# A hybrid RWKV-7 and attention block on one core: the sums of squares of the down projections move to the place where these are projected, and the recurrence's output is split into a dead half of the hidden state during attention

## The chip, the core and the metric

The kernel runs on one core of a Trainium2 chip. The metric is device time in microseconds (us) from start to end of one execution. TensorE is called PE here, its weight loads PEld, VectorE DVE, ScalarE ACT, GpSimd POOL; SP is the engine that issues nearly all DMAs, and each engine works through its instructions in the order in which they stand in its own queue.

## What is computed

One layer on 256 latent tokens (`x`) and 256 context tokens (`ctx`), width 2048, everything in fp32. The lines of the reference that matter:

```python
hm = rmsnorm(h, norm_w) * (1 + scale) + shift          # per stream
rkv, z_r, wd, ad, q_dn, kv_dn, k_rope, z_m, gates = split_in(hm @ w_in)

# branch 1: RWKV-7 recurrence over the tokens, both directions, 16 heads -> o_rw (1024 wide)
# branch 2: multi-head latent attention, 8 heads
q  = (rmsnorm(q_dn, q_norm_w) @ w_uq)                  # q_dn is 512 wide
kv = (rmsnorm(kv_dn, kv_norm_w) @ w_ukv)               # kv_dn is 256 wide
k  = concat(k_nope, broadcast(k_rope))                 # k_rope is 64 wide
q, k = rmsnorm(q, q_gain), rmsnorm(k, k_gain)          # then rotary, softmax, o_ml = att * silu(z_m)

x_new = x + g * (sigmoid(g_r) * (o_rw @ w_br_r) + sigmoid(g_m) * (o_ml @ w_br_m)) @ w_out
```

Three row norms need sums of squares over rows of a down projection: of `q_dn`, of `kv_dn`, and of `k_rope` (as a part of the norm of `k`). These sums are what the first half of the change moves.

## The kernel before

**Tiles and number format.** The hidden state `hm` lies transposed in SBUF, as 16 tiles of 128 features by 512 tokens (256 latent tokens in columns 0 to 255, 256 context tokens in columns 256 to 511). It is kept as a pair of fp32r tensors, a rounded high part `hmh` and the remainder `hml`. Every weight block is loaded (`w`, 128x1024, three buffers), and each half of it split in the same way by ACT (`wh`, a cast) and DVE (`wl`, a subtraction), three buffers each. A product is then three matmuls (`mm3`, line 221): high by high, high by low, low by high. `acc<-hmh,wh` and its two sisters in the profile are such matmuls of the input projection; below they are called projection matmuls. All recorded work runs through two helper classes, so nearly every instruction has the line L103 (matmul), L107 (transpose) or L122 (elementwise).

**Stages.** (1) Modulation, norm and the first six projection tiles. (2) The recurrence of branch 1: two chains of small steps (`front_chain` and `back_chain`) with finishing steps and a block inversion as further queues. `drive` (line 505) writes them in the order in which a small clock model expects their operands, and whenever no chain is ready it advances a generator `bg` (line 1032), the background, by one step. The background holds the rest of the input projection: the tiles that the recurrence needs next, and then the list `extra`: 24 tiles of merge gates, two tiles of `kv_dn` (`kv_g`, line 470), `k_rope` (`kr_g`, line 479), four tiles of `q_dn` (`q_g`, line 475), eight of `z_m` (`zm_g`) and the last eight merge gates. A background step is two to six projection matmuls. (3) Attention, lines 1077 to 1336, in six stages. Stage 0 runs `down()` (line 1135), stages 1 to 4 `up(hp)` for a pair of heads (queries, keys and values), stages 2 to 5 `attend(hp)` for the pair that `up` finished one stage earlier. In each round every generator of the stage takes a step, and then the background takes on average `BGM = 1.3` steps (`BG0 = 8` in stage 0). So projection matmuls fill PE's waits in all stages until they run out. (4) The merge: o_rw and o_ml by `w_br`, tile by tile, gated and summed. (5) The product with `w_out` and the residual.

**What `down()` does.** While it projects, the kernel writes the down projections to DRAM: `spill` (line 464) copies 256 columns from PSUM with ACT into a tile `th` (tag `th`, two buffers, shared with all the other generators) and lets SP store it to `kvd`, `krd` or `qdd`. `krd` has 128 rows, since `kr_g` leaves two partial sums in the upper and lower 64 partitions. After the recurrence, `down()` loads `kvr`, both halves of `krd` and `qdr`, adds the halves on DVE, squares everything on ACT into a double-buffered tile `sq`, and sums over the features with 20 small matmuls into one PSUM tile `pss` (each takes 128 columns of `sq` as its weights and two columns of ones as its data). From `pss` come the row norms: an inverse square root by integer tricks and three Newton steps on DVE (`rsqrt`, 11 small instructions), then `spread`, which multiplies a diagonal matrix `dg` by ones to bring the norms onto all partitions. With them `kvr` is scaled and split into `kvh`, `kvl`; `qdr` is scaled by its gain and split into `qnh`, `qnl`; and `krw` is transposed, rotated and doubled to `krS`.

**The end of the recurrence, and the merge.** The recurrence writes its output `y` per pair of heads to DRAM (`orwd`, 128x8x256). After attention the merge loads all of it (`orw`, two DMAs of 512 KB) and splits it into `ob0h`, `ob0l`, and `omla`, the attention's output, into `ob1h`, `ob1l`. Both are needed by the first merge tiles.

**What lies in the dead half.** After the last projection that reads context tokens, columns 256 to 511 of `hmh` and `hml` are not read as hidden state any more. `attend` keeps the transposed softmax weights `PT` there: head `hh` uses four of the 16 feature tiles, at `4 * (hh % 4)`.

Of the kernel before, what the change touches and what calls it, by code (L numbers as in the profile page):

```python
# [16 lines left out]
P = 128  # L17
# [109 lines left out]
def hybrid_block(  # L127
# [74 lines left out]
    def halfs(pool, shape, name, bufs=2):  # L202
        return [pool.tile(shape, F32R, name=name + c, tag=name + c, bufs=bufs) for c in "hl"]
# [247 lines left out]
    krd = dr1.tile([P, TT], F32, name="krd")  # L451
# [12 lines left out]
    def spill(dst, ps):  # L464
        th = wp.tile([P, T], F32, name="th", tag="th", bufs=2)
        t = th[0:dst.shape[0]]
        S.copy(t, ps)
        nc.sync.dma_start(dst, t)

    def kv_g(i):  # L470
        ps = yield from proj_g(76 + i, TT)
        for j in range(2):
            spill(kvd[:, i, T * j:T * j + T], ps[:, T * j:T * j + T])

    def q_g(i):
        spill(qdd[:, i], (yield from proj_g(72 + i, T)))
        done.add(("q", i))

    def kr_g():
# [16 lines left out]
        for j in range(2):  # L496
            spill(krd[:, T * j:T * j + T], ps[:, T * j:T * j + T])
# [52 lines left out]
    with tc.tile_pool(name="rw", bufs=1) as rw:  # L550
# [29 lines left out]
        def wk():  # L580
            return pp.tile([P, 512], F32, name="wk", tag="wk", bufs=2)
# [489 lines left out]
    omla = late.tile([P, 8, T], F32, name="omla")  # L1071


    with tc.tile_pool(name="ml", bufs=2) as ml:
# [60 lines left out]
        def down():  # L1135
# [3 lines left out]
            nc.sync.dma_start(krw, krd[0:64])  # L1139
            krw2 = ml.tile([64, TT], F32, name="krw", tag="Pm")  # L1140
            nc.sync.dma_start(krw2, krd[64:128])
            qdr = ml.tile([P, 4, T], F32, name="qdr", tag="vfl")
            nc.sync.dma_start(qdr, qdd)
            pss = wk()
            for k in range(2):
                sq = ml.tile([P, TT], F32, name="sq", tag="Pm")
                S.activation(sq, kvr[:, k], AF.Square)
                for i in range(4):
                    E.matmul(pss[:, 8 * k + 2 * i:8 * k + 2 * i + 2], lhsT=sq[:, 128 * i:128 * i + 128], rhs=ones[:, 0:2],
                             start=True, stop=True)  # L1150
            sq = ml.tile([P, TT], F32, name="sq", tag="Pm")
            V.tensor_tensor(krw, krw, krw2, ALU.add)
            S.activation(sq[0:64], krw, AF.Square)
            for i in range(4):
                E.matmul(pss[:, 16 + 2 * i:18 + 2 * i], lhsT=sq[0:64, 128 * i:128 * i + 128], rhs=ones[0:64, 0:2],
                         start=True, stop=True)
            for j in range(2):
                sq = ml.tile([P, 2, T], F32, name="sq", tag="Pm")
                S.activation(sq, qdr[:, 2 * j:2 * j + 2], AF.Square)
                for k in range(2):  # L1160
                    for i in range(2):
                        o = 24 + 4 * (2 * j + k) + 2 * i
                        E.matmul(pss[:, o:o + 2], lhsT=sq[:, k, 128 * i:128 * i + 128], rhs=ones[:, 0:2], start=True, stop=True)
            yield

            st = ml.tile([P, 40], F32, name="st", bufs=1)
            V.tensor_copy(st, pss[:, 0:40])
            s2 = st.rearrange("p (n two) -> p n two", two=2)[:, :, 0]
# [116 lines left out]
        def attend(hp):  # L1285
            qT, qrT, kT, vf, rq, rkb = ups.pop(hp)
            for h in range(2):
# [6 lines left out]
                b = 4 * (hh % 4)  # L1294
# [30 lines left out]

        due = 0.0
        for stage in range(6):
            us = [down()] if stage == 0 else [up(stage - 1)] if stage < 5 else []
            at = [attend(stage - 2)] if stage > 1 else []
            gs = us + at  # L1330
# [184 lines left out]
```

## Time and profile before

| | |
|---|---|
| median of three runs | 1336.67 us (1335.77 to 1337.12) |
| the profiled execution's own time | 1337.52 us |
| its span in the trace | 1335.6 us |
| its mean granted PE clock | 0.981 |
| recurrence | to about 969 us of the span |
| `down()` and attention | about 970 to 1143 us |
| merge | about 1144 to 1244 us |
| last product | to the end |

How to read it: the span runs from the first to the last recorded instruction; the 1.9 us between it and the execution's own time lie around it and are not in any row. "PEclk" and the clock in the rows by stretch are the share of full speed that was granted to PE. A row of the timeline gives the start, the time, the engine, the tiles and, in brackets, how long the engine was idle before it and what ended that. Matmul rows overlap, since they are pipelined: what one costs is the distance from one start to the next.

### The profile page before, as it was taken

Reading aid. Unit: us, or ns where it says so; the run is one execution under the profiler, and the core shown is the slowest. Engines: PE = TensorE matmul, PEld = TensorE weight load, DVE = VectorE, ACT = ScalarE, POOL = GpSimd, SP = SyncE. Lnnn points to the kernel's source line nnn. Section 1 sums busy time; section 2 is a strip of 40 time slices with the busy share of each in tenths; the row PEclk is TensorE's granted clock in tenths of the full one; section 3 lists DMA queues with packets and bytes.
Section 4 is the critical chain, followed back from the end, with each engine's and each line's share of the span. In section 5 each row is a group of like instructions: output and inputs, shape, how many; then the busy total and the mean of one; then the engine's idle time right before and its main releaser. Section 6 shows DMA issues by size and latency. Waiting matters only on the chain.

```text
span 1335.6 us, 29638 instructions
## 1 busy us (share of the span) xinstructions
PE 1273.5 (95%) x11484; PEld 1057.0 (79%) x11484; DVE 958.0 (72%) x2704; ACT 618.8 (46%) x1370; POOL 3.3 (0%) x9
## 2 busy tenths in 40 slices
PE   5999989999999998999999999999989999799998
PEld 2667877788787787788787777788878888799887
DVE  4445878878777868677876887776548877677655
ACT  3445544444443544344444444544436665444443
POOL 0000000000000000000000000000000000000000
PEclk9999999999999999999999999999979999899999
DMA  9995554354352454254254232353344332577685
GB/s 380 417 418 206 181 164 130 89 171 142 78 173 64 123 163 127 56 166 132 57 110 125 72 99 80 93 151 100 107 150 123 103 103 95 189 227 234 188 270 174
DMA packets 127740, 208.12 MB, mean 156 GB/s; under 512 B 63600, under 2 KB 80752, under 8 KB 127088
## 3 DMA queue, kind: packets, MB, share of 16 engines
q1 hardware_dynamic: 127600, 206.23, 49.0%
q8 instruction: 90, 1.47, 0.5%
q14 instruction: 50, 0.41, 0.1%
HBM read 193.33 MB, written 12.85 MB: 154 GB/s over the span
## 4 chain that ended last, share of the span: by engine, by line
PE 79%; DVE 11%; DMA 6%; issue 2%; ACT 2%; SPq 0%; DVEq 0%; ACTq 0%
PE acc L103 33%; PE chp L103 17%; PE lv L103 10%; PE wk L103 6%; PE a L103 5%; PE ch L103 3%; DMA w<-in_w_proj 3%; DVE wl L122 3%; PE wk L107 2%; PE pm L103 2%; DMA wm<-in_w_mod_ss 2%; DVE BK L122 1%; ACT wh L122 1%; DVE wt L122 1%; DMA xT<-in_xcT 1%
## 5 line engine op out<-in xcount | busy, mean ns | idle before, releaser
L122 ACT CAST wh<-w 128x512 fp32r<-128x512 f32 (+1 forms) x484 | 289.1, 607 | 336.3 <-PE acc L103 182.5
L122 DVE TENSOR_TENSOR wl<-w,wh 128x512 fp32r<-128x512 f32 (+1 forms) x480 | 319.7, 674 | 134.1 <-ACT wh L122 123.8
L103 PE MATMUL acc<-hmh,wh 128*128 128x256 f32 (+1 forms) x1200 | 390.6, 325 | 0.0
L103 PE MATMUL acc<-hml,wh 128*128 128x256 f32 (+2 forms) x1200 | 370.3, 309 | 0.8 <-issue 0.8
L103 PE MATMUL acc<-hmh,wl 128*128 128x256 f32 (+1 forms) x1184 | 364.6, 308 | 0.6 <-DVE wl L122 0.5
L103 PEld LDWEIGHTS acc<-hmh,wh 128*128 128x128 f32 x1200 | 228.0, 190 | 28.7 <-issue 6.8
L103 PEld LDWEIGHTS acc<-hmh,wl 128*128 128x128 f32 x1184 | 225.3, 190 | 14.9 <-DVE wl L122 1.1
L103 PEld LDWEIGHTS acc<-hml,wh 128*128 128x128 f32 (+1 forms) x1200 | 228.0, 190 | 11.0 <-issue 0.8
L122 DVE TENSOR_TENSOR pr<-wt 64x14 f32<-64x14 f32 (+6 forms) x224 | 42.5, 190 | 4.7
L122 DVE TENSOR_TENSOR wt<-wt,pr 64x14 f32<-64x14 f32 (+6 forms) x224 | 42.3, 189 | 4.3
L122 ACT COPY UV<-Mn 64x128 f32<-64x128 f32 x112 | 33.1, 295 | 22.1 <-DVE Mn L122 18.4
L103 PE MATMUL chp<-ob0h,wh 128*128 128x256 f32 x128 | 37.4, 293 | 5.7 <-ACT ob0h L122 5.7
L103 PEld LDWEIGHTS chp<-UV,AQ 128*64 128x64 f32 (+1 forms) x512 | 24.5, 138 | 21.3 <-ACT UV L122 10.9
L103 PE MATMUL a<-hmh,wh 128*128 128x512 f32 x96 | 40.7, 424 | 0.0
L122 ACT COPY UV<-chp 64x128 f32<-64x128 f32 x64 | 16.5, 257 | 50.8 <-PE chp L103 50.6
L103 PE MATMUL chp<-UV,AQ 128*64 128x64 f32 (+1 forms) x512 | 35.9, 238 | 4.2 <-ACT UV L122 4.1
L103 PE MATMUL a<-hmh,wl 128*128 128x512 f32 x96 | 38.1, 397 | 0.4 <-DVE wl L122 0.4
L103 PE MATMUL a<-hml,wh 128*128 128x512 f32 x96 | 37.9, 395 | 0.0
L103 PE MATMUL chp<-ob0l,wh 128*128 128x256 f32 x128 | 37.4, 292 | 0.0
L122 DVE SCALAR_TENSOR_TENSOR Mn<-chp,rho,Mr 128x64 f32<-128x64 f32 x96 | 24.1, 278 | 18.2 <-PE chp L103 17.7
L103 PE MATMUL chp<-ob0h,wl 128*128 128x256 f32 x128 | 37.1, 290 | 0.0
L103 PE MATMUL chp<-ob1h,wh 128*128 128x256 f32 x128 | 36.5, 285 | 0.0
(324 smaller groups left out, 2388.1 us busy)
## 6 DMA issues: line engine op xcount, KB each, us to landing
w<-in_w_proj SPq DMA_DIRECT2D x148, 512.0 KB, 3.8
wm<-in_w_mod_ss SPq DMA_DIRECT2D x64, 512.0 KB, 9.4
w<-in_w_mod_g SPq DMA_DIRECT2D x32, 512.0 KB, 3.6
w<-in_w_br SPq DMA_DIRECT2D x32, 512.0 KB, 3.6
w<-in_w_out SPq DMA_DIRECT2D x32, 512.0 KB, 3.7
w<-in_w_first SPq DMA_DIRECT2D x16, 384.0 KB, 8.5
xT<-in_xcT SPq DMA_DIRECT2D x4, 1024.0 KB, 8.6
thd<-th SPq DMA_DIRECT2D x32, 128.0 KB, 1.8
```

What stands on the lines that cost most here:

```text
L103: return self.engine.matmul(out, lhsT=lhsT, rhs=rhs, **kw)
L107: return self.engine.transpose(*a)
L122: return fn(out, *a, **kw)
```

## The change

The sums of squares are taken at the place where the tiles are projected. `spill` becomes a generator: after the copy and its store it squares the same PSUM columns with ACT into a second `th` tile, yields, sums with two small matmuls per 256 columns into a PSUM tile `wk`, and copies four columns into a tile `sqd` that stays in SBUF. `kr_g` first adds its two partial sums (a copy of the upper 64 partitions into a `th` tile, an addition in PSUM on DVE), so that `krd` has 64 rows and one load. `down()` then only loads, and starts with the norms from `sqd`.

The split of the recurrence's output moves from the merge into attention. A new generator `bring()` runs beside `up(2)` and `attend(1)` in stage 3: eight times it loads 128x256 of `orwd` into a `th` tile and splits it into feature tiles 8 to 15 of the dead half. To make room, `attend` uses `4 * (hh % 2)`. The merge reads branch 1 from there (in the profile these merge matmuls are then `chp<-hmh,wh`) and keeps only the split of `omla`.

```diff
-    krd = dr1.tile([P, TT], F32, name="krd")
+    krd = dr1.tile([64, TT], F32, name="krd")
+
+    sqd = cst.tile([P, 40], F32, name="sqd")
...
-    def spill(dst, ps):
+    def spill(dst, ps, col):
+
         th = wp.tile([P, T], F32, name="th", tag="th", bufs=2)
-        t = th[0:dst.shape[0]]
-        S.copy(t, ps)
-        nc.sync.dma_start(dst, t)
+        n = dst.shape[0]
+        S.copy(th[0:n], ps)
+        nc.sync.dma_start(dst, th[0:n])
+        sq = wp.tile([P, T], F32, name="th", tag="th", bufs=2)
+        S.activation(sq[0:n], ps, AF.Square)
+        yield
+        pss = pp.tile([P, 512], F32, name="wk", tag="wk", bufs=2)
+        for i in range(2):
+            E.matmul(pss[:, 2 * i:2 * i + 2], lhsT=sq[0:n, 128 * i:128 * i + 128], rhs=con("ones")[0:n, 0:2], start=True, stop=True)
+        V.tensor_copy(sqd[:, col:col + 4], pss[:, 0:4])
...
         for j in range(2):
-            spill(krd[:, T * j:T * j + T], ps[:, T * j:T * j + T])
+            ts = slice(T * j, T * j + T)
+            low = wp.tile([P, T], F32, name="th", tag="th", bufs=2)
+            S.copy(low[0:64], ps[64:P, ts])
+            V.tensor_tensor(ps[0:64, ts], ps[0:64, ts], low[0:64], ALU.add)
+            yield from spill(krd[:, ts], ps[0:64, ts], 16 + 4 * j)
...
+    ob = [[t[:, 8:16, T:TT] for t in (hmh, hml)]]
...
-            nc.sync.dma_start(krw, krd[0:64])
-            krw2 = ml.tile([64, TT], F32, name="krw", tag="Pm")
-            nc.sync.dma_start(krw2, krd[64:128])
+            nc.sync.dma_start(krw, krd)
...
-            pss = wk()
-            for k in range(2):
-                sq = ml.tile([P, TT], F32, name="sq", tag="Pm")
-                S.activation(sq, kvr[:, k], AF.Square)
...
-            V.tensor_copy(st, pss[:, 0:40])
-            s2 = st.rearrange("p (n two) -> p n two", two=2)[:, :, 0]
+            s2 = sqd.rearrange("p (n two) -> p n two", two=2)[:, :, 0]
...
-                b = 4 * (hh % 4)
+                b = 4 * (hh % 2)
...
+        def bring():
+
+            for p in range(8):
+                th = wp.tile([P, T], F32, name="th", tag="th", bufs=2)
+                nc.sync.dma_start(th, orwd[:, p])
+                yield
+                split(th, *(t[:, p] for t in ob[0]))
+                yield
...
-            gs = us + at
+            gs = us + at + ([bring()] if stage == 3 else [])
...
-    ob = [halfs(mg, [P, 8, T], f"ob{b}", 1) for b in range(2)]
-    orw = mg.tile([P, 8, T], F32, name="orw", bufs=1)
-    for b in range(2):
-        for q in range(2):
-            qs = slice(4 * q, 4 * q + 4)
-            if not b:
-                nc.sync.dma_start(orw[:, qs], orwd[:, qs])
-            split((omla if b else orw)[:, qs], ob[b][0][:, qs], ob[b][1][:, qs])
+    ob.append(halfs(mg, [P, 8, T], "ob", 1))
+    for q in range(2):
+        qs = slice(4 * q, 4 * q + 4)
+        split(omla[:, qs], *(t[:, qs] for t in ob[1]))
```

**How the instructions stand now.** Three places carry the prediction.

ACT's queue in the recurrence, where the first `kv_dn` tile is spilled (`th` is the spill's tile, `acc` its PSUM source, `UV`, `Y`, `wt` belong to the recurrence's chains), before:

```order
L122 CAST wh<-w 128x512
L122 COPY th<-acc 128x256 x2
L122 COPY UV<-chp 64x128
L122 CAST wh<-w 128x512
L122 COPY wt<-wt 64x256
```

Both copies stand in a row here, one in each of the two `th` buffers. The same place of ACT's queue in the changed kernel, where `ACTIVATE th<-acc` is the new square:

```order
L122 CAST wh<-w 128x512
L122 COPY th<-acc 128x256
L122 ACTIVATE th<-acc 128x256
L122 COPY UV<-chp 64x128
L122 COPY th<-acc 128x256
L122 COPY Y<-chp 128x128
L122 ACTIVATE th<-acc 128x256
L122 COPY wt<-wt 64x256
```

The second copy now needs the buffer whose store to DRAM began only two instructions earlier, and `Y` and `wt` of the recurrence stand behind it.

DVE's queue at the end of the recurrence and in `down()`, before (`krw` is the addition of the two halves, `st` the copy of the sums, `ss` the start of the norms):

```order
L122 TENSOR_TENSOR wl<-w,wh 128x512
L122 SCALAR_TENSOR_TENSOR th<-th,acc 128x256
L122 TENSOR_TENSOR krw<-krw 64x512
L122 TENSOR_SCALAR qdr<-qdr,vv 128x256 x3
L122 COPY st<-wk 128x40
L122 TENSOR_SCALAR qdr<-qdr,vv 128x256
L122 TENSOR_TENSOR wl<-w,wh 128x512 x2
L122 TENSOR_TENSOR ss<-st 128x4
```

The norms begin after all the loads and sums. DVE's queue at the same place in the changed kernel, where the norms (`rs`) are nearly done:

```order
L122 TENSOR_TENSOR wl<-w,wh 128x384
L122 SCALAR_TENSOR_TENSOR rs_y<-rs_z,rs_y 128x6
L122 SCALAR_TENSOR_TENSOR th<-th,acc 128x256
L122 TENSOR_TENSOR wl<-w,wh 128x512
L122 SCALAR_TENSOR_TENSOR rs_z<-rs_y 128x6
L122 TENSOR_TENSOR rs_z<-rs_z,ss 128x6
L122 SCALAR_TENSOR_TENSOR rs<-rs_z,rs_y 128x6
L122 TENSOR_TENSOR rs_12592<-rs 128x2
L122 TENSOR_TENSOR dg<-cc,rs 128x512
L122 TENSOR_SCALAR qdr<-qdr,vv 128x256 x4
L122 SCALAR_TENSOR_TENSOR kvr<-kvr,vv,wk 128x512 x2
L122 TENSOR_TENSOR qnl<-qdr,qnh 128x1024
```

The norms moved ahead of everything that waits for a load; PE's `spread` of `dg` now follows 92 projection matmuls after the last transposes of the recurrence (`chp<-cc,rvb`), where 102 stood there ahead of the first sums before.

ACT's queue for the last pair of heads, before (`Pm` is the exponential, `hmh` the copy of transposed weights into the dead half, `wh` the split of a weight block for projection or merge matmuls):

```order
L122 CAST wh<-w 128x512
L122 ACTIVATE Pm,sm<-Pm,sm 128x512
L122 CAST wh<-w 128x512
L122 ACTIVATE Pm,sm<-Pm,sm 128x512
L122 CAST hmh<-wk 128x4x128
L122 CAST wh<-w 128x512
L122 ACTIVATE th<-acc 128x256
L122 CAST hmh<-wk 128x4x128
```

Weight splits stand between the softmax steps, so PE has projection matmuls to do. ACT's queue at the same place in the changed kernel:

```order
L122 CAST qrTh<-wk 128x512
L122 ACTIVATE Pm,sm<-Pm,sm 128x512 x2
L122 CAST hmh<-wk 128x4x128 x2
L122 ACTIVATE Pm,sm<-Pm,sm 128x512 x2
L122 CAST hmh<-wk 128x4x128 x2
L122 CAST obh<-omla 128x1024
L122 CAST wh<-w 128x512
```

No weight split is left between them: stage 3 has more rounds than before, since `bring()` takes 16 steps, each round takes background steps, and the background is used up when the last pair of heads begins. Before, 64 projection matmuls stood in PE's queue from the last `dg` to the end of attention; now none does there, but 24 merge matmuls of branch 1 follow the last pair.

More of the change, by code (lines that the diff above doesn't have):

```diff
@@ L472, in kv_g @@
         for j in range(2):
-            spill(kvd[:, i, T * j:T * j + T], ps[:, T * j:T * j + T])
+            yield from spill(kvd[:, i, T * j:T * j + T], ps[:, T * j:T * j + T], 8 * i + 4 * j)
     def q_g(i):
-        spill(qdd[:, i], (yield from proj_g(72 + i, T)))
+        yield from spill(qdd[:, i], (yield from proj_g(72 + i, T)), 24 + 4 * i)
         done.add(("q", i))
@@ L1138, in down @@
             krw = ml.tile([64, TT], F32, name="krw", tag="Pm")
-            nc.sync.dma_start(krw, krd[0:64])
-            krw2 = ml.tile([64, TT], F32, name="krw", tag="Pm")
-            nc.sync.dma_start(krw2, krd[64:128])
+            nc.sync.dma_start(krw, krd)
             qdr = ml.tile([P, 4, T], F32, name="qdr", tag="vfl")
             nc.sync.dma_start(qdr, qdd)
-            pss = wk()
-            for k in range(2):
-                sq = ml.tile([P, TT], F32, name="sq", tag="Pm")
-                S.activation(sq, kvr[:, k], AF.Square)
[L1148 to L1163, printed above, removed]
             yield
-            st = ml.tile([P, 40], F32, name="st", bufs=1)
-            V.tensor_copy(st, pss[:, 0:40])
-            s2 = st.rearrange("p (n two) -> p n two", two=2)[:, :, 0]
+            s2 = sqd.rearrange("p (n two) -> p n two", two=2)[:, :, 0]
             V.tensor_tensor(ss[:, 0:4], s2[:, 0:4], s2[:, 4:8], ALU.add)
```

## Prediction

> **What bounds the kernel now.** I read the page's busy times first, then what PE waited for, then the two places where its clock falls.
>
> ```profile
> PE 1273.5 (95%) x11484; PEld 1057.0 (79%) x11484; DVE 958.0 (72%) x2704; ACT 618.8 (46%) x1370; POOL 3.3 (0%) x9
> PEclk9999999999999999999999999999979999899999
> ```
>
> PE is busy for 95% of the span, so PE's work and what stops or slows PE set the time. PE's clock falls in two of the 40 slices: at `down()` and where the merge begins. Both are what the change touches. PE's longest wait in each place (total, times, longest):
>
> ```profile
> PE wk L103 <- issue: 2.7, 1, 2.7
> PE chp L103 <- ACT ob0h L122: 5.7, 1, 5.7
> ```
>
> The clock costs more than the waits. PE alone, by stretch: length, busy time and records, granted clock, DMA.
>
> ```profile
> 977.35:980.76 3.41, 0.71 (x7) 1.00 1.00 332
> 980.76:984.17 3.41, 3.40 (x16) 0.50 0.92 347
> 991.00:994.41 3.41, 2.50 (x10) 0.50 0.00 0
> 994.41:997.83 3.42, 3.37 (x14) 0.50 0.50 141
> 997.83:1001.24 3.41, 3.41 (x20) 1.00 0.03 12
> 670.15:673.56 3.41, 1.91 (x17) 1.00 0.45 97
> 1141.19:1144.60 3.41, 1.64 (x12) 1.00 0.21 79
> 1144.60:1148.01 3.41, 0.00 (x0) 0.50 0.91 292
> 1151.43:1154.84 3.41, 3.41 (x18) 0.50 0.35 129
> ```
>
> The clock changes on a grid of 3.41 us. Stretches busy for 21% and 48% are followed by half clock, one busy for 56% is not; 73% busy at half clock does not bring it back, a full stretch does. The Trainium skill (TensorE: Matmul & The Clock Gate, Part 1, "What's actually happening") says half rate comes after an idle window of about 3.4 us and full rate after a busy one. The grid agrees; that a window has to be idle does not, since 48% busy lost the clock.
>
> **`down()` loses its sums.** The first three rows are PE's records in 978.06 to 998.20 on projection tiles, on `sq` and on `lv`; the last gives the price of a projection matmul.
>
> ```profile
> 978.06:998.20 20.14, 4.85 (x19) 0.58 0.39 135
> 978.06:998.20 20.14, 9.14 (x40) 0.58 0.39 135
> 978.06:998.20 20.14, 1.49 (x5) 0.58 0.39 135
> 966.44:978.06 11.62, 11.62 (x102) 1.00 0.78 230
> ```
>
> Of these 20.14 us the changed kernel still has to do 19 projection matmuls at 11.62 / 102 = 0.114 and four `lv` matmuls (the fifth only begins at the edge), of 384 columns instead of 256 and so at about 0.18: 2.9 us. What goes is 17.2 us: idle PE, 20 sums at half clock, and the rest at half clock. **-17.2.**
>
> **The sums come back in the recurrence.** The nearest row is a sum of the same form, `ysq`, between two projection matmuls.
>
> ```profile
> 960.96 0.28 PE L103 MATMUL acc<-hmh,wl 128*128 128x256 f32 x1
> 961.15 0.61 PE L103 MATMUL chp<-cc,ysq 128*128 128x2 f32 x4
> 961.62 0.36 PE L103 MATMUL acc<-hmh,wh 128*128 128x256 f32 x1
> 800.00:890.00 90.00, 88.29 (x938) 72.82 (x934) 68.19 (x204) 42.79 (x106) 0.00 (x0) 0.98 0.36 104
> kvd<-th SPq DMA_DIRECT2D x4, 128.0 KB, 1.8
> ```
>
> Two sums put 0.66 us between two projection matmuls that stand 0.11 apart otherwise: 0.55. Ten spills make 5.5 us. The recurrence's stretch that holds them (800 to 890, PE's busy time is the second number) has 1.7 us of idle PE, so between 3.8 and 5.5 is paid; I take 5.5, since the chains, and not the sums, choose when PE is idle. Then there are new waits: `kv_g` and `kr_g` each spill twice in quick succession, and the second copy on ACT waits until the store from its `th` buffer has landed, 1.8 us after its issue; `Y` and `wt` of the recurrence, and the next weight split, stand behind it. Two or three split weight halves of 12 or 24 projection matmuls cover some 2 us for PE. Without that cover it is four waits of about 1 us: 0 to 4, I take 1, near the covered end, because ACT is busy for 42.79 of the 90 us only. `sqd`'s copies (four columns) and the squares hide beside PE, since both engines have room in that row. **+6.5, from 3.8 to 9.5.**
>
> **What is late next in `down()`.** Nothing there waits for a sum any more; it waits for loads and for DVE.
>
> ```profile
> 973.93 0.58 SPq L1143 DMA_DIRECT2D qdr<-qdd  x1
> DMA to landing us min/median/max: 6.3/6.3/6.3
> 974.58 2.29 DVE L122 TENSOR_TENSOR wl<-w,wh 128x384 fp32r<-128x384 f32 x4 [1.52 <-ACT wh L122]
> 979.33 0.68 DVE L122 TENSOR_TENSOR krw<-krw 64x512 f32<-64x512 f32 x1 [2.13 <-DMA krw<-krd]
> 988.77 0.62 DVE L122 TENSOR_SCALAR qdr<-qdr,vv 128x256 f32<-128x256 f32 x2 [8.76 <-ACT sq L122]
> 993.84 1.04 ACT L122 CAST qnh<-qdr 128x1024 fp32r<-128x1024 f32 x1 [1.43 <-DVE qdr L122]
> 1003.67 0.15 DVE L122 TENSOR_TENSOR rs<-rs 128x2 f32<-128x2 f32 x1
> 1003.75 0.69 DVE L122 TENSOR_TENSOR dg<-cc,rs 128x512 f32<-128x512 f32 x1
> ```
>
> In before's times: 92 projection matmuls after the transposes end at 966.44 + 92 x 0.114 = 976.9. The `dg` stands behind the four weight splits, which end at 976.9 because a weight load lands at 974, and behind one `th` (0.4), some five small steps (0.15 to 0.2 each) and itself (0.7): about 979.0. `krw` lands at 979.3 at the latest, sooner now by the second `krw` load, gone from the queue. PE idles 2.1 us. Then `spread`, the transposes and 11 projection matmuls run to 981.7. `qdr` is there at 973.9 + 6.3 = 980.2; four scalings (1.2) and `qnh` (1.0) end at 982.4 if it lands then, at 982.0 with one load fewer: 0.3. `qnl` stands behind two scalings of `kvr` (0.7 each) and takes 1.2: 0.5; the next weight splits behind it: 0.5; the rotation of `krw`: 0.3. Sum 3.7 us idle, from 2 (loads sooner) to 7 (a weight load late in SP's queue behind `kvr`, `krw`, `qdr` and a store of `zmd`, which waits for DVE). The first gap loses the clock if 1.7 of its 2.1 us lie in one window: (3.41 + 2.1 - 2 x 1.7) / 3.41, 6 of 10 positions of the grid, taking the grid's place as chance; one window at half costs 1.7, two cost 3.4: 1.3 on the mean. **+5.0, from 2 to 10.**
>
> **The merge.**
>
> ```profile
> 1143.20 0.42 DVE L122 SCALAR_TENSOR_TENSOR omla<-gm,chp 128x256 f32<-128x256 f32 x1 [1.66 <-PE chp L103]
> 1143.65 4.09 DMA orw<-orwd
> 1148.86 0.58 PE L103 MATMUL chp<-ob0h,wh 128*128 128x256 f32 x1 [5.70 <-ACT ob0h L122]
> L122 ACT CAST ob1h<-omla x2: 1039/1042/1044, 1143.7 to 1144.7; 128x1024 fp32r<-128x1024 f32 x2
> L122 DVE TENSOR_TENSOR ob1l<-omla,ob1h x2: 1220/1222/1225, 1144.8 to 1145.9; 128x1024 fp32r<-128x1024 f32 x2
> ```
>
> The chain of waits runs through the load of `orw` and its split: 5.7 us of idle PE, then 6.0 us at half clock (1148.86 to the edge at 1154.84), 3.0 lost. Now 18 merge matmuls of branch 1 follow at once (18 x 0.114 = 2.1 us), while `omla` and the first half of its split take 0.4 + 1.0 + 1.2 = 2.7: 0.7 idle. Clock losses go into the last term. -8.7 + 0.7 = **-8.0.**
>
> **`bring()` in stage 3.**
>
> ```profile
> 1056.00:1089.00 33.00, 32.83 (x223) 29.42 (x223) 26.41 (x77) 20.92 (x48) 0.00 (x0) 1.00 0.33 102
> ```
>
> Eight casts on ACT and as many subtractions on DVE, each of a quarter of the columns of `ob1h`'s and at about the 0.42 of `omla`'s row: some 3.3 us on each engine, in a stage where DVE idles 6.6 us of 33 (third busy time) and ACT 12. Eight loads join SP's queue, and each waits for one of two `th` buffers with weight loads and gate loads behind it; the three weight buffers cover that. If neither cover holds it is 3.3. Nothing is removed in this stage, so nothing is gained. **+0.6, from 0 to 3.3.**
>
> **The last pair of heads has no filler.** The rows: before's stretch from the last `dg`, a score's last matmul, the first product with the values behind it.
>
> ```profile
> 1119.49:1143.17 23.68, 9.55 (x66) 1.00 0.32 103
> 1125.42 0.39 PE L103 MATMUL chp<-krS,qrTl 128*128 128x512 f32 x1
> 1136.30 0.39 PE L103 MATMUL chp<-krS,qrTl 128*128 128x512 f32 x1
> 1140.88 0.39 PE L103 MATMUL chp<-hmh,vfh 128*128 128x256 f32 x1 [0.68 <-ACT hmh L122]
> ```
>
> From the end of a head's second score (1136.69) to its first value product is 4.2 us of maximum, exponential, normalization, transposes and split on DVE and ACT; the first score lies 1.2 ahead, and DVE takes the first tile's steps between (0.2). So 5.6 us pass from first score to values, in which PE has 1.2 + 2 x 0.5 us of work now. With values, next head's score (2.5) and the second head to its end (5.6 + 2.1) that is 15.8 us, where before took 1143.17 - 1125.81 = 17.4; ahead of it stood eight more projection matmuls, 0.9, of which about 0.5 is saved. The stretch shrinks by 2.1 us, but its 64 projection matmuls (7.3 us) were done earlier: +5.2 idle, from 4 to 7. Clock: per head, 3 us idle of about 4.5; windows that begin from 0.2 before to 2.6 after the first score's end hold 1.7 us of idle PE, 8 of 10 positions, and 73% at half does not restore the clock. One loss costs 1.7 to 3.4; two, the second running into the merge: 3.5, from 1.5 to 6. **+8.7, from 5.5 to 13.**
>
> **Sum.** -17.2 + 6.5 + 5.0 - 8.0 + 0.6 + 8.7 = -4.4. The profiled execution took 1337.5, 0.9 over the median: 1333.1, or **1332.3** against the median of 1336.67.
>
> **Rivals.**
> *Slower: the `th` buffers.* All spills, the gates and `bring()` share two. If a spill held the recurrence's chain on ACT or the `wk` PSUM tiles that its front half needs, PE would wait up to 1.8 us for each of ten. 7 us decide, 0.7 a spill; at 1.1 a spill the time is 1332.3 - 1 + 11 = 1342. For it: `Y`, `wt` and weight splits stand behind the second copy. Against it: the idle 1.7 us in 90.
> *No change: half clock through the whole last pair.* PE's 9 us of work there take 18, of which the idle time hides about half, and the merge starts at half: some 5 more, 1337.3. For it: five stretches in a row at half in `down()`. Against it: the value products and scores between are a full stretch.
> *No change: the loads hold `down()` as long.* If they land 5 us later: 1337. Against it: DMA idles after 984.
> *Much faster: the clock holds.* Without both clock terms, 1.3 + 3.5 less: 1327.5. For it: the stretch at 56%, which held; the new gaps come in pieces of 0.3 to 2.1 us. Against it: the stretch at 48%, which did not. The rule of the Trainium skill's page above, taken as it stands, speaks for this rival, since no gap here is a whole idle window.
>
> **How the numbers follow.** A measurement of this kernel can tell about 0.2%, 2.7 us, from no change: faster is below 1334.0, slower above 1339.3. The forecast has 0.58 (0.50 of it faster, 0.08 same; own range 1329.5 to 1335.3), the `th` rival 0.10 (slower), half clock throughout 0.15 (0.14 same, 0.01 slower), the loads 0.03 (same), the clock that holds 0.14 (faster): 0.64, 0.25, 0.11. The range 1326.5 to 1338.5 leaves out the `th` rival and the far ends of the others.
>
> **What would show it.** Right: `sq` gone from PE's waits after the recurrence, an idle PE of about 4 us between the transposes and `krS`; ten `wk` sums in 800 to 900; no wait of 5 us ahead of the merge; new PE waits on `Pm`, `hmh` for the last two heads, with half clock there. Wrong: PE waits on `th`, `UV` or `wk` of several us in the recurrence, or full clock in the last pair.

## The result, and the profile after

The changed kernel takes 1328.7 us (median of five runs, 1327.3 to 1333.0), the kernel before beside it 1337.1 (1335.8 to 1341.8). The ratio is 0.9936, interval 0.9911 to 0.9961: 8.4 us less, with 5 to 12 in the interval. The profiled execution took 1329.92 us, its span is 1328.1. Forecast were 1332.3 us, in a range of 1326.5 to 1338.5.

The page of the changed kernel, engines and granted clock in 40 slices:

```profile
PE 1271.5 (96%) x11484; PEld 1053.2 (79%) x11484; DVE 961.1 (72%) x2720; ACT 620.2 (47%) x1383; POOL 3.3 (0%) x9
PEclk9999989999999999899999999999999999999999
```

The slice of `down()`, a 7 before, is a 9 now (90% or more), and so is the one where the merge begins, an 8 before. To see where the time went I cut both spans at the same five events: first spill, last transposes of the recurrence, first score on `krS`, last `dg`, last `omla`, end. PE alone; length, busy time and records, clock, DMA share, GB/s. Before:

```profile
799.70:966.20 166.50, 164.16 (x1839) 0.99 0.37 105
966.20:1031.10 64.90, 57.96 (x367) 0.87 0.45 141
1031.10:1118.30 87.20, 86.83 (x585) 1.00 0.32 99
1118.30:1143.20 24.90, 23.49 (x162) 1.00 0.33 101
1143.20:1335.60 192.40, 182.29 (x1152) 0.97 0.69 219
```

After:

```profile
802.10:976.70 174.60, 173.79 (x1892) 1.00 0.36 104
976.70:1023.10 46.40, 42.81 (x302) 1.00 0.58 184
1023.10:1119.60 96.50, 95.91 (x654) 1.00 0.38 115
1119.60:1144.30 24.70, 17.75 (x99) 0.93 0.10 32
1144.30:1328.10 183.80, 178.40 (x1146) 1.00 0.72 224
```

The lengths cannot be compared as they stand, since the background's projection matmuls are not in the same stretches: 667, 203, 190, 76 and none before, 697, 187, 250, 5 and none after. With 0.114 us for each of them (the prediction's price) the stretches read, at equal numbers of projection matmuls:

| stretch | length, after less before | projection matmuls | at equal projection matmuls | forecast |
|---|---|---|---|---|
| to the first spill | +2.4 | about equal | +2.4 | 0 |
| recurrence from the first spill | +8.1 | +30 | +4.7 | +6.5 |
| to the first score (`down()`) | -18.5 | -16 | -16.7 | -17.2 + 5.0 = -12.2 |
| stages to the last `omla` | +9.1 | -11 | +10.4 | +0.6 + 8.7 = +9.3 |
| merge and last product | -8.6 | 0 | -8.6 | -8.0 |

No edit touches the part ahead of the first spill, except that 14 small chain matmuls stand ahead of it and two projection matmuls behind it. In the fourteen traces of this case it ends anywhere between 792.4 and 802.1 us, at 799.6 us in another execution of the changed kernel; so I count the first row as scatter, whose cause is open. Other matmuls changed places too: seven of the first queries (`lv`, 384 columns, 0.18 us each) and two of the first scores (0.23 each), 1.7 us in all, stand ahead of the first score on `krS` before and behind it after, and eight merge matmuls (0.9 us) stand ahead of the last `omla` after. With these the third row is -15.0, the fourth +7.8 and the fifth -7.7.

What PE waited for in the two places, `down()` and then the last pair with the merge (total, times, longest):

```profile
PE wk L103 <- issue: 1.4, 1, 1.4
PE wk L107 <- DVE kr L122: 1.2, 1, 1.2
PE wk L107 <- DVE Pm L122: 4.3, 4, 1.5
PE chp L103 <- ACT hmh L122: 2.0, 3, 0.7
PE chp L103 <- DVE obl L122: 0.7, 1, 0.7
```

No wait on `sq` is left in `down()`, and the 5.7 us ahead of the merge are 0.7, on the split of `omla`. In exchange PE waits 6.3 us for the softmax of the last four tiles and its transposed weights: in 1119.60 to 1144.30 it does 99 matmuls and is idle for 6.95 us, where it did 162 and was idle for 1.41.

### The profile page after: what moved, and what is told of

It reads as the page before. It is cut to its first block, busy times and chain, and to the rows that moved or that the text cites. A ratio compares the mean times of both kernels' runs of the same rounds, so it can differ in the third digit from the quotient of the medians.

```text
span 1328.1 us, 29671 instructions
## 1 busy us (share of the span) xinstructions
PE 1271.5 (96%) x11484; PEld 1053.2 (79%) x11484; DVE 961.1 (72%) x2720; ACT 620.2 (47%) x1383; POOL 3.3 (0%) x9
## 4 chain that ended last, share of the span: by engine, by line
PE 79%; DVE 10%; DMA 6%; ACT 2%; issue 2%; SPq 1%; DVEq 0%; ACTq 0%
PE acc L103 33%; PE chp L103 17%; PE lv L103 10%; PE wk L103 6%; PE a L103 5%; PE ch L103 3%; DVE wl L122 2%; DMA w<-in_w_proj 2%; PE wk L107 2%; PE pm L103 2%; DMA wm<-in_w_mod_ss 2%; DVE BK L122 1%; ACT wh L122 1%; DMA xT<-in_xcT 1%; DVE wt L122 1%
## 5 line engine op out<-in xcount | busy, mean ns | idle before, releaser
L122 ACT ACTIVATE Mr<-Mn,rho 128x64 f32<-128x64 f32 x96 | 30.1, 342 | 15.7 <-DVE Mn L122 14.6
L103 PE MATMUL chp<-obl,wh 128*128 128x256 f32 x128 | 36.4, 284 | 0.7 <-DVE obl L122 0.7
L103 PE MATMUL chp<-hmh,wh 128*128 128x256 f32 x128 | 36.2, 283 | 0.0
L103 PE MATMUL chp<-hmh,wl 128*128 128x256 f32 x128 | 36.2, 283 | 0.0
```

Of the source, the lines that this page charges most:

```text
L103: return self.engine.matmul(out, lhsT=lhsT, rhs=rhs, **kw)
L122: return fn(out, *a, **kw)
```

## The experiments

They ran on four chips, on each of which the kernel before takes 1333.1 to 1334.7 us, not 1337; so ratios to before on the same chip are compared. The last column counts the projection matmuls that stand in PE's queue between head 7's second score and head 8's first, between head 8's two, and behind those: the filler of the last pair.

| kernel | median us | ratio to before | interval | filler at the end |
|---|---|---|---|---|
| before (its own BGM, 1.3) | 1333.1 to 1334.7 | 1 | | 25, 11, 18 |
| `r1_after`: the change again | 1326.3 | 0.9954 | 0.9937 to 0.9970 | 0, 0, 0 |
| `e1_sums`: first half alone | 1328.3 | 0.9965 | 0.9954 to 0.9975 | 24, 0, 0 |
| `e2_bring`: second half alone | 1330.8 | 0.9983 | 0.9972 to 0.9994 | 10, 0, 0 |
| `e3_nine`: `bring()` in nine steps | 1321.0 | 0.9911 | 0.9892 to 0.9931 | 24, 0, 0 |
| `e4_nosum`: the sums left out | 1326.4 | 0.9955 | 0.9940 to 0.9969 | 0, 0, 0 |
| `e7_twice`: the sums done twice | 1327.7 | 0.9958 | 0.9943 to 0.9973 | 0, 0, 0 |
| `e5_nine12`: nine steps, BGM 1.2 | 1317.2 | 0.9881 | 0.9862 to 0.9899 | 24, 6, 18 |
| `e6_bgm11`: the change, BGM 1.1 | 1316.3 | 0.9887 | 0.9868 to 0.9906 | 27, 2, 3 |
| `e8_nosum10`: no sums, BGM 1.0 | 1311.4 | 0.9830 | 0.9816 to 0.9843 | 24, 2, 10 |
| `e9_bring115`: second half, BGM 1.15 | 1323.0 | 0.9912 | 0.9898 to 0.9925 | 24, 2, 20 |
| `e10_chain12`: statistics earlier, BGM 1.2 | 1317.8 | 0.9877 | 0.9862 to 0.9892 | 24, 4, 18 |
| `e11_before115`: before, BGM 1.15 | 1326.0 | 0.9951 | 0.9932 to 0.9971 | 27, 5, 60 |

BGM is the number of background steps per round of the stages. A trace shows one execution, which can lie off its median: that of `r1_after` took 1330.3 us, of `e4_nosum` 1322.9, of `e6_bgm11` 1321.0, of `e10_chain12` 1321.2 and of `e11_before115` 1321.6. Part of this lies ahead of the first spill, so traces are compared by stretch, and gains are taken from the ratios.

### Each half alone

The first half is the changed kernel with the merge, the load of `orw` and `attend`'s four places as before; the second is the kernel before with these lines of the diff:

```diff
+    ob = [[t[:, 8:16, T:TT] for t in (hmh, hml)]]
...
-                b = 4 * (hh % 4)
+                b = 4 * (hh % 2)
...
+        def bring():
...
-            gs = us + at
+            gs = us + at + ([bring()] if stage == 3 else [])
...
+    ob.append(halfs(mg, [P, 8, T], "ob", 1))
```

Expected of the first:

> The changed kernel's first half alone: the sums of squares at the projections, while the recurrence's output is loaded and split at the merge, as before. By the prediction's own terms: -17.2 + 6.5 + 5.0 = -5.7 against before, 1331 us. By what the changed kernel's trace shows (recurrence some 5 to 7 us longer, the stretch from its end to the first score 16.7 shorter): -10 to -12, 1325 to 1327, less some 2 that the last head without filler gives back: 1327 to 1329. Rival, that the sums only moved and the merge brought the gain: 1336 to 1338.

Expected of the second:

> The second half alone: the recurrence's output joins h's dead half in stage 3, while the sums of squares are taken in the down projections' preparation, as before. By the prediction's own terms: -8.0 + 0.6 + 8.7 = +1.3, 1338 us. By the trace of the changed kernel (first score to last omla 10.5 longer, the rest 8.8 shorter): +1.7, 1338 to 1339. Rival, that the merge brought the gain: 1328 to 1330.

The first half is 4.7 us faster than before (1333.12 x 0.0035), interval 3.3 to 6.1: the prediction's terms gave 5.7, the reading of the changed kernel's trace 8 to 10, which is too much; why its rows promised more is open, since no profile of the kernel before was taken on this chip. The second half is 2.3 us faster (0.8 to 3.7), where both readings had it slower. Together they make 7.0, close to the 6.1 that the whole change is worth in `r1_after`. So the gain does not lie in the merge alone. The second half alone, last pair and then merge to the end:

```profile
1120.00:1146.30 26.30, 21.78 (x119) 0.87 0.16 51
1146.30:1329.00 182.70, 176.93 (x1146) 0.99 0.70 225
```

It still has 119 matmuls in its last pair (99 in the changed kernel) and 4.5 us of idle PE: its recurrence takes 666 projection matmuls from the background and not 697, so the background lasts a little longer. `e1_sums`, which has no `bring()`, keeps 24, 0, 0 where before keeps 25, 11, 18. So both halves use up filler, and the price of the last pair belongs to what is left in the background there, and not to `bring()` as such.

### Where the filler is left

`e3_nine` loads and splits in nine steps, so that stage 3 goes round no oftener than without `bring()`; `e6_bgm11` leaves `bring()` as it is and changes the constant; `e5_nine12` has nine steps and the constant at 1.2.

```diff
-            for p in range(8):
-                th = wp.tile([P, T], F32, name="th", tag="th", bufs=2)
-                nc.sync.dma_start(th, orwd[:, p])
-                yield
-                split(th, *(t[:, p] for t in ob[0]))
-                yield
+            last = None
+            for p in range(9):
+                th = last
+                if p < 8:
+                    last = wp.tile([P, T], F32, name="th", tag="th", bufs=2)
+                    nc.sync.dma_start(last, orwd[:, p])
+                if p:
+                    split(th, *(t[:, p - 1] for t in ob[0]))
+                yield
```

> The changed kernel with bring() in nine steps (a load and the split of the part loaded one step earlier) in place of sixteen, so that stage 3 goes round no oftener than without it and releases no extra filler: 24 projection matmuls stand again between the scores of the last pair of heads. Theory that the last pair lacks filler: its 6.6 us of idle PE fall to about 4, the half clock there may go or stay: 2.5 to 5 us faster than the changed kernel, 1324 to 1326. Rival, that filler in the last pair only delays the heads' own chain, or that bring's casts then hold the weight splits: no difference, 1328 to 1330.

> The changed kernel with BGM at 1.1 in place of 1.3 and bring() in sixteen steps as it is: 27 and 2 projection matmuls stand between the last pair's scores, 3 behind them. Theory that only the filler's place matters: 3 to 5 us faster than the changed kernel, as nine steps were, 1320 to 1322 where before takes 1333. Rival, that the sixteen steps themselves cost in stage 3 (their loads ahead of weight loads, their casts ahead of weight splits): 1323 to 1325.

> bring() in nine steps, and BGM at 1.2 in place of 1.3, so that the stages release filler more slowly: 24 and 6 projection matmuls stand between the last pair's scores and 18 behind the values, ahead of the merge. Theory that PE's idle time behind the recurrence is a matter of where filler is left: the last pair idles about 1.5 us instead of 2.9 with nine steps alone and 6.95 in the changed kernel, and the 0.7 at the merge goes: 5 to 7 us faster than the changed kernel, 1318 to 1320 where before takes 1333. Rival, that the stages then lack the filler which the last pair gets: as nine steps alone, 1321, or slower.

The changed kernel itself was run beside the last two:

> The changed kernel once more, unaltered, so that it stands beside the others on one chip. By its measured ratio of 0.9936 [0.9911, 0.9961] to before: 1324.6 us where before takes 1333.1.

The last pair's stretch, last `dg` to last `omla`, in `r1_after`, `e3_nine`, `e6_bgm11` and `e5_nine12`:

```profile
1116.60:1144.70 28.10, 21.22 (x99) 0.77 0.09 28
1110.80:1136.70 25.90, 22.99 (x139) 0.89 0.18 56
1109.80:1135.20 25.40, 22.88 (x147) 0.93 0.25 78
1106.80:1130.90 24.10, 23.01 (x158) 1.00 0.26 83
```

From row to row PE does more matmuls in less time: idle 6.9, 2.9, 2.5 and 1.1 us, clock 0.77, 0.89, 0.93, 1.00. The stages before that do not pay for it: with BGM at 1.1 PE is idle for 0.4 us from the first score to the last `dg`. Against `r1_after`, BGM at 1.1 is worth 0.0067 x 1333 = 8.9 us, nine steps with BGM at 1.2 9.7, and nine steps alone 5.7, each with some 3.4 us of uncertainty either way. All three gained more than was expected of them, `e6_bgm11` beyond the uncertainty (3 to 5 expected); why is open. The prediction's term for the last pair was 8.7. The rival for `e6_bgm11`, that the sixteen steps cost something in stage 3, falls: it is as fast as `e5_nine12`. The rival for `e5_nine12`, that the stages would lack what the last pair gets, falls too: PE is idle for 0.7 us from its first score to its last `dg`.

### The price of the sums

In `e4_nosum` the sums are replaced by

```diff
-        pss = pp.tile([P, 512], F32, name="wk", tag="wk", bufs=2)
-        for i in range(2):
-            E.matmul(pss[:, 2 * i:2 * i + 2], ...)
-        V.tensor_copy(sqd[:, col:col + 4], pss[:, 0:4])
+        V.tensor_scalar(sqd[:, col:col + 4], con("ones")[:, 0:4], 64.0, None, ALU.mult)
```

and `e7_twice` does each matmul twice; `e8_nosum10` is `e4_nosum` with BGM at 1.0.

> The changed kernel without the twenty small sum matmuls in the recurrence: a constant is written where their sums went, the copies, squares and stores stay. By the price of the prediction (0.55 us for each of ten spills): 5.5 us faster than the changed kernel, 1323. Rival, that the sums fit beside the chains and cost what PE idles less there: 2 to 3 us, 1326. Rival, that the trace's other reading holds (PE's own busy time in the recurrence rose by 8.4 at equal work and clock): 8 us, 1320.

> The changed kernel with each of the twenty small sum matmuls done twice. By the price of the prediction a second pair costs no change of place, some 0.3 us for each of ten spills: 3 us slower than the changed kernel, 1327.6 where before takes 1333. Rival, that the price is one of PE's busy time and twice what was priced (the recurrence's busy time rose by 7.8 us at equal work): 5 to 8 slower, 1330 to 1333. Rival, that such work takes the place of filler and idle time: 0 to 1, 1325.

> The changed kernel without its twenty small sums (a constant is written where they went) and with BGM at 1.0, so that filler is left for the end: 24 and 2 projection matmuls between the last pair's scores, 10 behind them, about as in the changed kernel with BGM at 1.1 (27, 2 and 3). Theory that PE work saved in the recurrence counts in full once the last pair has filler: 5 to 6 us faster than the changed kernel with BGM at 1.1, 1310 to 1312 where before takes 1333. Rival, that the sums stand in the place of idle time and cost nothing: no difference from it, 1315 to 1318.

Neither leaving the sums out nor doubling them moved the changed kernel by anything measurable: 0.9955 and 0.9958 beside 0.9954. Each difference is known to some 3 us, so the 5.5 us expected of `e4_nosum` did not come, while the 3 us expected of `e7_twice` lie at the edge of what the times allow. The trace of `e4_nosum` shows where the time stayed: recurrence, stages to the last `dg`, last pair.

```profile
794.90:967.40 172.50, 169.62 (x1886) 1.00 0.37 109
1013.80:1110.90 97.10, 93.76 (x632) 0.99 0.35 112
1110.90:1136.90 26.00, 18.90 (x94) 0.84 0.02 6
```

PE is 4.2 us less busy in the recurrence, but there are 714 projection matmuls in it and not 697: the clock model that writes the order sees less work in a spill and fills the time with background. The background then ends 17 matmuls earlier; only 6 of them stand ahead of the last pair's first scores where the changed kernel has 24. PE is idle for 3.3 us in the stages (0.6 in the changed kernel) and for 7.1 in the last pair. What was saved early is given back late. The recurrence of `e7_twice` and of `e8_nosum10`:

```profile
796.60:971.50 174.90, 173.69 (x1920) 1.00 0.34 102
794.90:966.80 171.90, 169.44 (x1887) 1.00 0.37 109
```

With 684 and 715 projection matmuls in them, at 0.114 us each, the stretch is 1.8 us longer than in the changed kernel with the sums doubled, and 4.0 (`e4_nosum`) and 4.8 us (`e8_nosum10`) shorter without them. `e8_nosum10` has filler at its end, and there the time appears: 1311.4 us, 0.9830, against 0.9887 for `e6_bgm11`, which has the sums and much the same filler. That is 0.0057 x 1333 = 7.6 us, 4.5 to 10.7 with both intervals (half widths 0.0014 and 0.0019, as the root of the sum of their squares). So the sums cost about what was priced (4.0 to 4.8 us by the rows, 7.6 by the ratios), and leaving them out paid only where the end did not run dry. The changed kernel with its sums and BGM at 1.0 was not run, so part of the 7.6 us may be the constant's; against it stands `e5_nine12`, which has as much filler (24, 6, 18) and is no faster than `e6_bgm11`.

### The second half with filler, and a control

`e9_bring115` is `e2_bring`, and `e11_before115` the kernel before, with one line altered:

```diff
-BG0, BGM = 8, 1.3
+BG0, BGM = 8, 1.15
```

> The second half alone (the sums of squares in the down projections' preparation, as before; the recurrence's output joins h's dead half in stage 3) with BGM at 1.15 in place of 1.3: 24 and 2 projection matmuls between the last pair's scores and 20 behind them. By the prediction's terms without the last pair's, -8.0 + 0.6: 1325 to 1326 where before takes 1333. Rival, that the second half's worth lies elsewhere than in the merge's wait and the place of the filler does not matter: as with BGM at 1.3, 1330 to 1332.

> Control: the kernel before with BGM at 1.15 in place of 1.3 and nothing else; its last pair has 27 and 5 projection matmuls between the scores and 60 behind them (25, 11 and 18 with 1.3). Theory that the place of the filler matters only where the end runs dry: within 2 us of before. Rival, that a slower release is a gain of its own (which would explain the 9 us between the two forms of the second half alone): 4 to 8 us faster than before. A third way, that the 60 cover the load and split of orw ahead of the merge (5.7 us idle): up to 5 us faster, with the wait ahead of the merge shorter.

The second half with filler is 11.7 us faster than before (0.0088 x 1334.74; 10 to 14), where 7.4 less were expected. Its last pair and its merge:

```profile
1114.70:1138.30 23.60, 22.76 (x157) 1.00 0.27 89
1138.30:1320.90 182.60, 176.84 (x1146) 1.00 0.69 225
```

The first is 1.3 us shorter than before's, the second 9.8. The control is faster too, by 6.5 us (0.0049 x 1333; 4 to 9): outside what the first theory allowed. By its time it fits the rival as well as the third way. Its rows, the wait ahead of the merge, the stretch from the last `omla`, and two stretches of the clock's grid in it, bear out the third way:

```profile
PE chp L103 <- ACT ob0h L122: 3.3, 1, 3.3
1128.90:1319.80 190.90, 183.15 (x1182) 1.00 0.71 227
1130.63:1134.04 3.41, 1.60 (x15) 1.00 0.78 257
1134.04:1137.46 3.42, 1.89 (x15) 1.00 0.64 216
```

With 60 projection matmuls behind the last scores PE has work while `orw` is loaded and split: the wait falls from 5.7 to 3.3 us, and the clock holds at 1.00 where it was lost. That it held may be luck of this execution, since the two stretches are busy for 47% and 55%, and other traces lost the clock after such a share. Against before's trace, taken on another chip, and at equal projection matmuls (30 of them are in this stretch), the merge and last product are 4.9 us shorter, the last pair 1.7 and `down()` 2.0, but the stages between only 0.2: a slower release is no gain there, as the rival would have it. So the rule "filler matters only where the end runs dry" was too narrow: the load of `orw` is such a place too. One constant in the kernel before is worth about as much as the whole change in `r1_after`, and the change with its constant set again is worth more than twice as much (0.9887). The second half is then still worth 0.0039 (`e9_bring115` against `e11_before115`, both with BGM at 1.15), 5.2 us, and the first another 0.0025 (`e6_bgm11`, BGM 1.1, against `e9_bring115`), 3.3 us, though those two intervals overlap. Together that is 8.5 us between the two kernels with the constant set again in both; other values than 1.15 were not tried in the kernel before.

### The statistics earlier

`e10_chain12` takes one line out of `down()`, with BGM at 1.2:

```diff
             nc.sync.dma_start(qdr, qdd)
-            yield

             s2 = sqd.rearrange("p (n two) -> p n two", two=2)[:, :, 0]
```

> The changed kernel with the step's end ahead of the statistics taken out of down(), so that DVE's short steps and the spread of rs are written ahead of eight units of filler, and with BGM at 1.2 (24 and 4 projection matmuls between the last pair's scores, 18 behind them). Theory that PE's idle time in down() comes from the statistics queueing behind weight splits that wait for a load: 1 to 2 us less of it, 1314 to 1316 where before takes 1333 (1316.3 with BGM at 1.1 and the step's end). Rival, that PE then waits in front of the spread, with filler queued behind it: 2 to 4 us more idle time there, 1318 to 1320.

It is as fast as `e5_nine12` and `e6_bgm11`, which have the line (0.9877 beside 0.9881 and 0.9887), but not because nothing happens. Sixteen steps, BGM at 1.2 and the line were not run together, so the time alone does not decide between theory and rival. PE's longest wait in `down()`, the ACT instruction behind which it stood, and three stretches (all of `down()`, then two of the clock's grid):

```profile
PE acc L103 <- ACT wh L122: 3.0, 1, 3.0
985.24 1.04 ACT L122 CAST kvh<-kvr 128x1024 fp32r<-128x1024 f32 x1 [6.02 <-DVE kvr L122]
972.10:1017.20 45.10, 40.53 (x258) 0.92 0.50 164
983.39:986.80 3.41, 0.76 (x5) 1.00 0.98 376
986.80:990.22 3.42, 2.81 (x8) 0.50 0.33 83
```

The spread comes earlier, at 982.66, 10.7 us after the last transposes instead of 13.8 in the changed kernel, but ACT's queue now has the cast of `kvr` ahead of the next weight split, and ACT sits 6.0 us until `kvr` has landed and been scaled. PE then waits 3.0 us for that split, in one piece, and loses the clock as well. The saved wait came back as a longer one; the theory fails for this edit and the rival is right about the place, though the end of the kernel did not suffer: its `down()` takes 141 projection matmuls where that of `e6_bgm11` takes 181, so 40 are left for later stretches.

## Why the prediction was right, and which terms were off

**`down()` loses its sums (-17.2), and what is late next there (+5.0).** The mechanism was right; the second term was too large. In the stretch to the first score the two make -12.2, measured -15.0 (with the queries and scores that changed places). What holds `dg` is what the prediction named, the weight splits ahead of it and a weight load ahead of those. ACT, DVE and PE in `down()` of the changed kernel:

```profile
985.67 1.45 ACT L122 CAST wh<-w 128x384 fp32r<-128x384 f32 x3 [3.10 <-DMA w<-in_w_uq]
986.21 0.56 DVE L122 TENSOR_TENSOR wl<-w,wh 128x384 fp32r<-128x384 f32 x1 [1.94 <-ACT wh L122]
989.51 0.69 DVE L122 TENSOR_TENSOR dg<-cc,rs 128x512 f32<-128x512 f32 x1
990.12 1.14 DVE L122 TENSOR_SCALAR qdr<-qdr,vv 128x256 f32<-128x256 f32 x4
990.41 1.10 PE L103 MATMUL wk<-dg,cc 128*128 128x512 f32 x2 [1.36 <-issue]
```

`dg` ends at 990.2, 13.6 us after the last transposes (976.57); 13.0 were forecast. PE is idle for 2.1 us ahead of it, as forecast, but in pieces of 0.53, 0.25 and 1.36. The other 1.6 us, for `qdr`, `qnl` and the splits behind them, did not come: `qdr` was there when `dg` was, and PE had weight halves ready. Only the rotation of `k_rope` took more, 1.2. In all PE is idle for 3.6 us in the stretch, where the terms add up to 5.9 (6.9 before, less the 4.7 that were to go, and 3.7 new): 2.3 too many. The clock term, 1.3, is nought in this execution. The grid's stretches here and in the last pair:

```profile
986.48:989.90 3.42, 2.05 (x13) 1.00 0.58 158
989.90:993.31 3.41, 2.90 (x18) 1.00 0.84 303
1136.67:1140.08 3.41, 1.25 (x8) 1.00 0.00 0
1140.08:1143.49 3.41, 2.96 (x14) 0.50 0.00 0
```

The pieces leave the stretch of the gap 60% busy, and the clock stays; the stretch at 37% is followed by half clock. `e10_chain12` shows the other outcome: one piece of 3.0 us, a stretch at 22%, half clock after it.

**The sums in the recurrence (+6.5).** +4.7 in the rows, inside the stated 3.8 to 9.5; the price of the sums was right, and the waits that I had added did not come. The 40 records of the sums, alone:

```profile
799.00:892.00 93.00, 5.71 (x40) 1.00 0.35 98
```

5.7 us of PE's time for ten spills, 0.57 each, where 0.55 was taken from `ysq`. PE waits nowhere in the recurrence for `th` or for a `wk` tile that a sum holds, so the term of 1 us for that is nought and the rival of the `th` buffers (1342 us) is out. The stretch is 4.7 us longer at equal projection matmuls. Idle PE fell from 2.3 to 0.8 us, and the 1.7 us of clock that the execution before lost there (816.92 to 820.34) were not lost; so 2.2 us of the 4.7 are further busy time that no row here accounts for. That the term pays in full only if the end has filler is what the prediction did not see.

**The merge (-8.0).** -8.6 in the rows, -7.7 with the merge matmuls that stand ahead of the last `omla`. Six merge matmuls run among the last value products, 18 more follow these without a gap, and the split of `omla` costs 0.7 us, as forecast.

**`bring()` (+0.6).** PE waits for nothing in stage 3, 1040 to 1092, but 0.3 us for a `dg`. Its cost is the filler that its extra rounds take, which the prediction booked under the last pair.

**The last pair (+8.7).** 5.2 us more of idle PE were forecast; PE is idle for 6.95 us, 5.5 more than before. The clock term was 3.5, with 1.5 to 6 allowed: this execution lost one stretch, half of 2.96 us. The same kernel run again lost four, half of 12.3 us (its stretches of the grid; the first and the fourth, at full clock, are each followed by two at half):

```profile
1125.00:1128.41 3.41, 1.28 (x9) 1.00 0.05 16
1128.41:1131.82 3.41, 2.73 (x10) 0.50 0.00 0
1131.82:1135.24 3.42, 3.42 (x13) 0.50 0.00 0
1135.24:1138.65 3.41, 1.30 (x7) 1.00 0.00 0
1138.65:1142.06 3.41, 2.72 (x11) 0.50 0.00 0
1142.06:1145.48 3.42, 3.42 (x18) 0.50 0.00 0
```

That fits the argument that the size depends on where the grid lies, and both ends of the 1.5 to 6 us have been seen. The rival of a clock that holds falls, and with it the rule by which it would: the Trainium skill (TensorE: Matmul & The Clock Gate, Part 1, "What's actually happening") has half rate after an idle window, and no window here was idle. That the window runs freely, so that the same kernel meets it differently each time, is stated there too, and these two executions agree.

**The sum.** Forecast -4.4 in the profiled executions, measured -7.6; by medians -8.4, with 5 to 12 in the interval. 1328.7 us lies in the range of 1326.5 to 1338.5, but just outside the forecast's own 1329.5 to 1335.3, and nearer to the rival of a clock that holds (1327.5), whose mechanism did not happen. The signs named for right are all there. The term furthest off is "what is late next in `down()`", +5.0, which measured +2.2 (-15.0 beside -17.2): 1.3 us of new idle PE instead of 3.7, and no clock lost. The recurrence came out 1.8 lower, and the stages, with what changed places, 1.5 lower.

**What the prediction did not weigh** is the fixed amount of filler. It booked the last pair as a price of the second half. `e1_sums` and `e6_bgm11` show it as the price of a release rate that was set for another amount of work ahead of it, and a change of one constant takes it back.

## What to carry to other kernels

Where a fixed amount of background work hides the waits of a chain, an edit is worth what it leaves of that work for the last place that needs it: count it there before and after, in PE's queue, before pricing anything else. Here work saved early was worth nothing (`e4_nosum`) where it only pulled the background forward, and what was priced (`e8_nosum10`) where the release rate was set anew; so set the rate again after each change to the number of steps, and measure a change against a version of the old kernel with its rate set again as well (`e11_before115`). A wait that is taken away by writing its consumer earlier can come back as a longer one through the in-order queue of a third engine (`e10_chain12`).

## What the runs showed of the hardware that was not expected

The clock's grid has the same period, 3.413 us, in all fourteen traces, with a phase of its own in each. From the end of the recurrence on, every stretch of it at full clock in which PE was busy for 5% to 40% (14 of them) was followed by half clock, and every one above 57% by full clock; between 47% and 57% both occurred. The way back is less regular: at half clock no stretch up to 82% busy brought the full clock back, some of 84% to 89% did, and others of 91% to 100% did not. So the prediction's reading that a full stretch at half clock brings the full clock back does not hold: its own row at 980.76 is busy for 3.40 of 3.41 us, and half clock went on to 997.83. In this part of the kernel a gap is judged by its share of one stretch and not by its length: 2.1 us in three pieces left every stretch at least 60% busy and cost nothing (`down()` of the changed kernel), 3.0 us in one piece were followed by two stretches at half clock (`e10_chain12`). Earlier in the kernel the share does not decide; in the kernel before, a stretch of the recurrence in which PE is busy throughout is followed by half clock, and the cause is open:

```profile
813.50:816.92 3.42, 3.42 (x29) 1.00 0.00 0
816.92:820.34 3.42, 3.42 (x12) 0.50 0.00 0
```
